# Another written order of casts, splits and gates over the first fourteen steps of a one-core decoder layer, with three scratch stores asked for later

## The chip, the cores and the metric

The kernel runs on one core of a Trainium2 chip. A core has a matrix engine (TensorE, PE in the profile), a vector engine (VectorE, DVE), a scalar engine (ScalarE, ACT), GpSimd (POOL) and a sync engine (SyncE, SP) that here only issues transfers. Each engine works through its own list of instructions in order, and semaphores are all that binds one engine to another. Transfers (DMA) are asked for by SP, or by POOL where a transfer adds to what lies at its destination, and run on 16 shared DMA engines. The metric is the device time of one execution in microseconds, as the median of three runs.

## The reference

One decoder layer on 512 tokens of 1024 features, in float32: a SwiGLU feed-forward block (FFN), a token-mixing part, a second FFN and a gated embedding. The edited code is the entry of the first FFN, with the embedding's projection `p @ ple_w_proj` that is computed ahead of it:

```python
h = h + 0.5 * swiglu(rmsnorm(h, ffn1_norm), w_gate, w_up, w_down)     # 1024 -> 2816 -> 1024
...
gate = sigmoid(rmsnorm(h, ple_norm) @ ple_w_gate + ple_b_gate)
h = h + gate * (p @ ple_w_proj)
# swiglu(x, w_gate, w_up, w_down) = (silu(x @ w_gate) * (x @ w_up)) @ w_down
```

Every product is made of three matmul passes over high and low parts (`whi`, `wlo` of the weights, `xfa`/`xfb` of the input), so that float32 accuracy is kept.

## The kernel before

**Steps.** The program is a list of steps. A step is one product on PE with the work that feeds it and the work that follows it. For each step a weight block of 128x1024 is loaded, cast on ACT (`whi`, line 537) and subtracted on DVE (`wlo`, line 541); the two together are called a split, the first half the cast, the second the low half. The first matmul of a product waits for the cast, the third for the low half. There are three buffers for `whi` and three for `wlo`.

**The entry.** Steps 0 and 1 are the embedding's projection (line 1231). Steps 2 to 5 are a plain group of 256 of the 2816 inner columns (line 847, 24 matmuls of 512 columns each). From step 6 on, groups of 256 inner columns are computed in a form of Strassen's with seven products a group (line 753, 24 matmuls of 256 columns each). Group 1 has steps 6 to 11 and 13; group 2 begins with step 12 and goes on with 14, 15 and so on. Some weight blocks are sums of blocks: two are made by adding transfers from POOL (lines 768 and 771, into `raw` and `s1`), two by a DVE addition in place (line 763). Step 7 uses the `raw` that a POOL transfer added to, step 9 the sum `rawb + s1`, step 11 `s1`, step 13 the same `rawb` after a second addition.

**What follows a product.** The plain group's gate is formed by `plain_gate` (DVE line 869, ACT line 871, into `g`) and its result by `plain_finish` (DVE lines 877 and 879). In group 1, `gate_sum` (line 904) reads a finished accumulator and writes the gate buffer `G`; `gate` multiplies by the norm's factor (line 909) and applies silu on ACT (line 911); `times_r` (line 915) and `finish` (line 920) follow. The second `gate_sum` reads the accumulator `a` that step 11 has just finished, and step 13 writes into that same accumulator again, so step 13's first matmul waits for it.

**Other work in the entry.** The input is scaled and split into `xfa` and `xfb`, with sums and differences of blocks (lines 633 to 687). The norm's squares are taken from four row blocks of x (line 390), then a chain of small DVE instructions gives the factor per token (lines 240 to 246), and a product spreads it (line 343); ACT keeps it as `rall` (line 349). The embedding's eight tiles are copied out of the accumulators (line 1241) and stored to a scratch tensor `emb_dram` (line 1186). Their buffers `rawd` lie where `G` lies later, so the first write to `G` waits for the `rawd` stores to have landed.

**What sets the order.** PE, ACT, DVE and SP run in the order in which a planner (`run`) writes the instructions. For the entry, that order is a string, `ENTRY`: a name such as `split7` runs the cast and low half of step 7, `split7:1` only its next piece, `after11` what follows product 11, `load9` the transfers tied to step 9. A suffix `.1` or `.2` names a further task of that step. All tasks not named run afterwards in the planner's default order. Each engine's list is what is left of this sequence when the other engines' pieces are taken out.

Of the kernel before, what the change touches and what calls it, by code (L numbers as in the profile page):

```python
# [50 lines left out]
ENTRY = """  # L51
load0 load1 load1.1 load2 load3 load3.1 load4 load5 split0 split1 split1.1 load6 load6.1
product0 split2 load7 product1 after1:1 after0 split3 split3.1:6 split4.1:3 split3.1:1
split4.1:1 split3.1 split4.1 split5.1:1 load8 after1:1 product2 split4.2:1 split4.2:1 split5.1:1
after1 split4 split4.2 split6.2:2 load9 product3 split5:1 split5.2:1 split5 split5.1 split6.1
after4:1 split5.2 split6.2:1 after4 split6.2:1 split5.3 product4 split6 split6.2:1 split6.2
product5 after4.1 split7 split7.1 product6 split8:1 sums9 after5:1 split8 after6 after5:2
split9:2 split10.1:1 after5 product7 split10.1:1 split9 product8 split10.1:1 after7
split10 split10.1 load12 product9 split11 load14 product10 after9 after9.1 after10
after10.1:1 split12 product11 after11 split13  # L60
"""

BUFS = {
# [43 lines left out]
def layer_kernel(ctx: ExitStack, tc: tile.TileContext, a: dict, out: bass.AP):  # L107
# [7 lines left out]
    def open_pool(name, side):  # L115
        pools[name] = tc.alloc_tile_pool(name=name, bufs=1, side=side, reuse_waits="tile")
        home.update(dict.fromkeys(HOMES[name].split(), name))

    def close_pool(*names):
        for name in names:  # L120
            pools.pop(name).release()
# [362 lines left out]
    def listed(fns):  # L484
        return list(fns) if isinstance(fns, (list, tuple)) else [fns] if fns else []

    def also(step, what, fn):

        if what == "after":
            step.after = (listed(step.after[0] if step.after else ()) + [fn],) + tuple(step.after[1:])  # L490
        else:
            setattr(step, what, listed(getattr(step, what)) + [fn])
# [223 lines left out]
    def splitter(name, x):  # L716

        x += [None] * ND

        def done(d, tok=slice(0, T)):  # L720
            x[d] = scaled_split(h, name, d, tok, x[d])

        return done
# [457 lines left out]
    emb_dram = dram.tile([P, ND, T], F32, name="emb_dram", tag="emb_dram")  # L1181
    pe, stores = [], {}

    def store_embedding():
        for d in (4, 6, 0, 2, 3):
            nc.sync.dma_start(*stores[d])

    def embedding(q):
# [67 lines left out]
    steps, mix_norm = swiglu(  # L1256
        "ffn1", x_ffn1, ffn1_norm,
        lambda: (close_pool("ffn1_entry"), open_pool("ffn1_g", "left")),
        lambda: (close_pool("ffn1_g"), open_pool("mix_x", "left")),
        splitter("mix_norm", x_mix), 1,  # L1260
    )
    steps = [embedding(q) for q in range(2)] + steps
# [11 lines left out]

    also(steps[1], "split", lambda: Early.x(early, 0))
    also(steps[3], "split", lambda: Early.x(early, 1))
    also(steps[9], "load", store_embedding)
    also(steps[4], "split", lambda: Early.t(early, 3))
    also(steps[4], "split", lambda: Early.t(early, 2))
    also(steps[5], "split", lambda: ffn1_norm.add(0, 1, 2))  # L1280
# [607 lines left out]
    for n, d in enumerate(D_ORDER):  # L1888
# [11 lines left out]
    steps, ple_norm = swiglu(  # L1900
        "ffn2", x_ffn2, norm, lambda: open_pool("ffn2_g", "right"),
        lambda: (close_pool("ffn2_g"), open_pool("ple_x", "right")), splitter("ple_norm", x_ple), 0,
    )
# [297 lines left out]
```

## Time and profile before

| | us |
|---|---|
| median of 3 runs (lowest, highest) | 1015.03 (1014.21, 1016.19) |
| the profiled execution's own time | 1015.65 |
| its span, first to last instruction | 1013.9 |
| PE busy in the span | 1003.9 |
| DVE busy, ACT busy | 845.3, 580.6 |

The profile is one execution, with a page of totals and views of the trace. In a timeline row stand the start, the duration, the engine, the line, the operation, output and inputs by tile name, and the count of instructions; in square brackets the engine's idle time just ahead and what ended it. The granted TensorE clock is 1.000 in the whole span.

### The profile page before, as it was taken

To read this page: it belongs to the slowest core of one execution; us is meant where nothing else is said; L and a number is where in the kernel's file an instruction comes from. 1 tells how busy PE (TensorE), PEld (TensorE's weight loads), DVE (VectorE), ACT (ScalarE), POOL (GpSimd) and SP (SyncE) were. 2 spreads that over 40 slices of the span, in tenths; PEclk is the share of its full clock that TensorE was granted. 3 is DMA by queue.
4 is the path that set the end of the run, shared out by engine and by line. 5 is a ranking of instruction groups with operands and counts; after the bars stand their busy time and mean duration, and the time that the engine had idled before them with its cause. 6 is when DMAs were issued, how large, how long until landed. Compare 5 with 4: busy or idle time off the path is not lost.

```text
span 1013.9 us, 18331 instructions
## 1 busy us (share of the span) xinstructions
PE 1003.9 (99%) x7464; PEld 948.4 (94%) x7464; DVE 845.3 (83%) x1116; ACT 580.6 (57%) x783; POOL 134.5 (13%) x141
## 2 busy tenths in 40 slices
PE   9999999999999999999999999999999999999997
PEld 7899999999999899888888888899999999999987
DVE  7988888889988897776999757778888888988886
ACT  6755555556667474575754434455545546665765
POOL 0101001002311000144233100101011000330101
PEclk9999999999999999999999999999999999999999
DMA  8977767748972333444432233746777756995512
GB/s 334 330 205 206 197 193 205 207 146 223 205 176 64 95 114 98 152 154 131 130 121 84 104 104 130 216 120 186 201 208 194 181 167 207 215 211 137 167 63 84
DMA packets 51333, 168.90 MB, mean 167 GB/s; under 512 B 5808, under 2 KB 6576, under 8 KB 51248
## 3 DMA queue, kind: packets, MB, share of 16 engines
q1 hardware_dynamic: 39584, 125.71, 36.2%
q0 software_dynamic: 11520, 41.95, 22.3%
q8 instruction: 58, 0.95, 0.4%
q14 instruction: 27, 0.22, 0.1%
q10 hardware_dynamic: 144, 0.07, 0.0%
HBM read 163.44 MB, written 4.26 MB: 165 GB/s over the span
## 4 chain that ended last, share of the span: by engine, by line
PE 88%; DVE 6%; DMA 3%; issue 1%; ACT 1%; SPq 0%; DVEq 0%; ACTq 0%
PE mm L753 20%; PE a L753 15%; PE a L1139 8%; PE mm L231 6%; PE sm L217 6%; PE mm L1139 5%; PE sm L1139 5%; PE mm L217 5%; PE sm L231 4%; PE a L217 4%; PE a L231 3%; DVE wlo L541 1%; DMA s<-in_ffn_gu 1%; DMA raw<-in_ffn_gu 1%; PE sm L847 1%
## 5 line engine op out<-in xcount | busy, mean ns | idle before, releaser
L541 DVE TENSOR_TENSOR wlo<-raw,whi 128x1024 fp32r<-128x1024 f32 (+2 forms) x162 | 199.4, 1231 | 58.3 <-ACT whi L537 58.1
L537 ACT CAST whi<-raw 128x1024 fp32r<-128x1024 f32 (+2 forms) x162 | 166.2, 1031 | 135.5 <-DVE raw L763 30.6
L753 PE MATMUL mm<-xfb,whi 128*128 128x256 f32 x960 | 163.9, 275 | 0.0
L753 PEld LDWEIGHTS mm<-xfb,whi 128*128 128x128 f32 x960 | 145.5, 192 | 0.0
L753 PE MATMUL mm<-xfb,wlo 128*128 128x256 f32 x480 | 132.1, 275 | 0.2 <-DVE wlo L541 0.2
L537 ACT CAST whi<-rawb 128x1024 fp32r<-128x1024 f32 x76 | 79.6, 1048 | 63.3 <-DVE rawb L763 29.5
L541 DVE TENSOR_TENSOR wlo<-rawb,whi 128x1024 fp32r<-128x1024 f32 x76 | 92.9, 1222 | 21.5 <-ACT whi L537 20.9
L753 PE MATMUL a<-xfb,whi 128*128 128x256 f32 x640 | 109.4, 275 | 0.0
L753 PEld LDWEIGHTS a<-xfb,whi 128*128 128x128 f32 x640 | 97.0, 192 | 0.0
L753 PEld LDWEIGHTS mm<-xfb,wlo 128*128 128x128 f32 x480 | 92.2, 192 | 0.4 <-DVE wlo L541 0.4
L753 PE MATMUL a<-xfb,wlo 128*128 128x256 f32 x320 | 88.1, 275 | 0.0
L1139 PE MATMUL a<-xfb,whi 128*128 128x256 f32 x480 | 80.7, 275 | 0.0
L1139 PEld LDWEIGHTS a<-xfb,whi 128*128 128x128 f32 x480 | 73.0, 192 | 0.0
L768 POOL DMA_DIRECT2D raw<-in_ffn_gu x20 | 17.3, 864 | 398.5 <-DMA raw<-in_ffn_gu 154.5
L217 PE MATMUL sm<-x,whi 128*128 128x512 f32 x224 | 68.3, 387 | 0.0
L1139 PE MATMUL a<-xfb,wlo 128*128 128x256 f32 x240 | 66.0, 275 | 0.0
L911 ACT ACTIVATE G<-G 128x512 f32<-128x512 f32 x40 | 25.3, 633 | 65.4 <-DVE G L909 64.1
L753 PEld LDWEIGHTS a<-xfb,wlo 128*128 128x128 f32 x320 | 61.4, 192 | 0.1
L753 PE MATMUL a<-xfa,whi 128*128 128x256 f32 x320 | 54.7, 275 | 0.1
L753 PE MATMUL mm<-xfa,whi 128*128 128x256 f32 x320 | 54.8, 275 | 0.0
L1139 PE MATMUL mm<-xfb,whi 128*128 128x256 f32 x320 | 53.8, 275 | 0.0
L1139 PE MATMUL sm<-xfb,whi 128*128 128x256 f32 x320 | 53.8, 275 | 0.0
(428 smaller groups left out, 2604.6 us busy)
## 6 DMA issues: line engine op xcount, KB each, us to landing
raw<-in_ffn_gu SPq DMA_DIRECT2D x56, 512.0 KB, 4.9
rawb<-in_ffn_gu SPq DMA_DIRECT2D x32, 512.0 KB, 8.8
raw<-in_w_in SPq DMA_DIRECT2D x28, 512.0 KB, 3.6
s<-in_ffn_gu SPq DMA_DIRECT2D x20, 512.0 KB, 5.7
raw<-in_ffn_gu POOLq DMA_DIRECT2D x20, 512.0 KB, 5.8
s<-in_ffn_gu POOLq DMA_DIRECT2D x20, 512.0 KB, 9.7
rawb<-in_ffn_dw POOLq DMA_DIRECT2D x18, 512.0 KB, 7.9
raw<-in_w_out SPq DMA_DIRECT2D x16, 512.0 KB, 3.2
```

The source lines that it names most:

```text
L217: nc.tensor.matmul(ps, w, turned(x), start=first and n == 0, stop=last and n == 2, skip_group_check=True)
L231: nc.tensor.matmul(ps[:, tok], wt[:, c], turned(xt[:, tok]), start=first and k == i == 0, stop=last and k == len(xs) - 1 and i == len(by_p ...
L537: nc.scalar.copy(self.hi[:, c], self.raw[:, c])
L541: nc.vector.tensor_tensor(self.lo[:, c], self.raw[:, c], self.hi[:, c].bitcast(F32), ALU.subtract)
L753: nc.tensor.matmul(o, wt[:, c], turned(xt), start=fresh and p == m == n == 0, stop=last and n == 2, skip_group_check=True,)
L768: nc.gpsimd.dma_start(w21.raw, self.src[0], accum_op=ALU.add)
L847: nc.tensor.matmul(ps, (whi, whi, wlo)[n][:, c], t[:, 0:2, n % 2].rearrange("p s (b i) -> p s i b", b=2), start=not lower and p == n == 0, ...
L911: nc.scalar.activation(t, t, AF.Silu)
L1139: nc.tensor.matmul(o, wt[:, c], xt, start=i in (1, 7) and t == jj == n == d % 2 == 0, stop=t == nt - 1 and jj == 1 and d % 2 == 1 and n == ...
```

## The change

The string `ENTRY` is rewritten from step 1's place to step 13's. The products stand in the same order. On ACT and DVE the splits of steps 4 to 9 and of step 12 and 13 are written earlier relative to the work around them: relative to the norm's squares, to the last of the input's sums (`split5.3`), to the plain group's gate (`after5`) and finish (`split10.1`), and to group 1's gates (`after10`, `after11`). Of the five stores to `emb_dram`, the two of 256 KB stay with step 9's loads, and the other three of 512 KB are tied to step 14's loads (`load14.1`) instead. No instruction is added or taken away.

```diff
-split4.1:1 split3.1 split4.1 split5.1:1 load8 after1:1 product2 split4.2:1 split4.2:1 split5.1:1
-after1 split4 split4.2 split6.2:2 load9 product3 split5:1 split5.2:1 split5 split5.1 split6.1
-after4:1 split5.2 split6.2:1 after4 split6.2:1 split5.3 product4 split6 split6.2:1 split6.2
-product5 after4.1 split7 split7.1 product6 split8:1 sums9 after5:1 split8 after6 after5:2
-split9:2 split10.1:1 after5 product7 split10.1:1 split9 product8 split10.1:1 after7
-split10 split10.1 load12 product9 split11 load14 product10 after9 after9.1 after10
-after10.1:1 split12 product11 after11 split13
+split4.1:1 split3.1 split4.1 split5.1:1 load8 after1:1 product2 split4.2:1 split4.2:1 split4
+split5.1:1 after1 split4.2 split6.2:2 load9 product3 split5:1 split5.2:1 split5 split5.1 split6.1
+after4:1 split6.2:1 split6:1 after4 split6.2:1 split6 product4 split6.2 split5.2 split5.3:1
+product5 after4.1 split7:1 split8:1 split5.3:1 split7 split8 split7.1 product6 sums9 after5:1 after6
+split9 split5.3 after5:2 product7 split10 after7 after5 split10.1:2 product8 split11:1 load12 split11
+product9 after9 split12:1 split12 split10.1 load14 load14.1 product10 after9.1 split13:1 after10 split13
+after10.1:1 product11 after11
...
-    def store_embedding():
-        for d in (4, 6, 0, 2, 3):
+    def store_embedding(*ds):
+        for d in ds:
             nc.sync.dma_start(*stores[d])
...
-    also(steps[9], "load", store_embedding)
+    also(steps[9], "load", lambda: store_embedding(2, 3))
+    also(steps[14], "load", lambda: store_embedding(4, 6, 0))
```

What the rewritten string makes of the engines' lists is shown at three places. The first is ACT ahead of step 4, as a piece of the difference; `whi_318` was and `whi_314` is the cast of step 4's weights, and line 390 takes the squares of a row block of x.

```order
 L390 ACTIVATE whix_174,rtok_281<-whix_174 128x1024
 L1241 COPY rawd_250<-mm_223 128x512
+L537 CAST whi_314<-raw_140 128x1024
 L390 ACTIVATE wlox_176,rtok_281<-wlox_176 128x1024
-L537 CAST whi_318<-raw_140 128x1024
 L668 CAST xfb_100<-ghi_271 128x512
```

Step 4's cast now stands ahead of the second row block's squares instead of behind them.

The second place is DVE from step 11's low half (`wlo_588` before, `wlo_557` now) to step 14's (`wlo_697` in both), with the semaphores that each row waits for. First the list before, in which `wlo_634` is step 12's low half and `wlo_663` step 13's:

```order
L541 TENSOR_TENSOR wlo_588<-s_57_217,whi_587 128x1024 [waits PE_49,Activation_49]
L763 TENSOR_TENSOR rawb_172<-rawb_172,rawb_283 128x1024
L904 TENSOR_TENSOR G_630<-mm_503,u_116_623 128x2x256 [waits DMAHW4_49,DMAHW5_49,PE_49,Activation_49]
L909 SCALAR_TENSOR_TENSOR G_630<-G_630,rall_489 128x2x256 [waits DVE_49]
L541 TENSOR_TENSOR wlo_634<-raw_110_561,whi_633 128x1024 [waits DMAHW1_49,Activation_49]
L904 TENSOR_TENSOR G_630<-a_98_459,p_107_554 128x2x256 [waits PE_49]
L541 TENSOR_TENSOR wlo_663<-rawb_172,whi_662 128x1024 [waits Activation_49]
L915 SCALAR_TENSOR_TENSOR G_630<-G_630,rall_489 128x2x256 [waits Activation_49]
L541 TENSOR_TENSOR wlo_697<-raw_591,whi_696 128x1024 [waits DMASW2_49,Activation_49]
```

Then the list now, in which `wlo_589` is step 12's low half and `wlo_631` step 13's; DMAHW3 and DMAHW2 are the semaphores of the two `rawd` stores:

```order
L541 TENSOR_TENSOR wlo_557<-s_57_217,whi_556 128x1024 [waits PE_49,Activation_49]
L541 TENSOR_TENSOR wlo_589<-raw_112_559,whi_588 128x1024 [waits DMAHW6_49,PE_49,Activation_49]
L877 SCALAR_TENSOR_TENSOR g_487<-g_487,rall_485 128x512
L879 TENSOR_TENSOR g_487<-g_487,a_82_332 128x512 [waits DVE_49]
L763 TENSOR_TENSOR rawb_172<-rawb_172,rawb_283 128x1024
L904 TENSOR_TENSOR G_637<-mm_498,u_113_586 128x2x256 [waits DMAHW3_49,DMAHW2_49,PE_49]
L541 TENSOR_TENSOR wlo_631<-rawb_172,whi_630 128x1024 [waits Activation_49]
L909 SCALAR_TENSOR_TENSOR G_637<-G_637,rall_485 128x2x256 [waits DVE_49]
L904 TENSOR_TENSOR G_637<-a_100_458,p_109_527 128x2x256 [waits PE_49]
L915 SCALAR_TENSOR_TENSOR G_637<-G_637,rall_485 128x2x256 [waits Activation_49]
L541 TENSOR_TENSOR wlo_697<-raw_594,whi_696 128x1024 [waits DMASW2_49,Activation_49]
```

Step 12's low half moved ahead of the plain group's finish (lines 877, 879), of the second addition (line 763) and of the first gate sum; step 13's low half moved ahead of line 909 and of the second gate sum, the line-904 row that reads the accumulator `a`.

The third place is SP's list of transfers, before:

```order
L511 DMA rawb_283<-in_ffn_gu 128x1024
L1186 DMA emb_dram<-rawd_250 128x1024
L1186 DMA emb_dram<-rawd_315 128x1024
L1186 DMA emb_dram<-embt_252 128x1024
L1186 DMA emb_dram<-p_65_255 128x512
L1186 DMA emb_dram<-u_66_257 128x512
L511 DMA raw_110_561<-in_ffn_gu 128x1024
L511 DMA raw_591<-in_ffn_gu 128x1024
L770 DMA s_114_594<-in_ffn_gu 128x1024
L511 DMA raw_597<-in_ffn_gu 128x1024
L511 DMA rawb_667<-in_ffn_gu 128x1024
```

and now:

```order
L1186 DMA emb_dram<-p_65_255 128x512
L1186 DMA emb_dram<-u_66_257 128x512
L511 DMA raw_112_559<-in_ffn_gu 128x1024
L511 DMA raw_594<-in_ffn_gu 128x1024
L770 DMA s_117_597<-in_ffn_gu 128x1024
L511 DMA raw_600<-in_ffn_gu 128x1024
L1186 DMA emb_dram<-rawd_250 128x1024
L1186 DMA emb_dram<-rawd_319 128x1024
L1186 DMA emb_dram<-embt_252 128x1024
```

The three large stores moved behind group 2's first four loads; the last of these, `raw_600`, overwrites the buffer that step 7's split reads.

## The prediction

> **What bounds the kernel now.** I read the page's totals first, then the chain of waits, then the stretches of the entry.
>
> ```profile
> span 1013.9 us, 18331 instructions
> PE 1003.9 (99%) x7464; PEld 948.4 (94%) x7464; DVE 845.3 (83%) x1116; ACT 580.6 (57%) x783; POOL 134.5 (13%) x141
> PE 88%; DVE 6%; DMA 3%; issue 1%; ACT 1%; SPq 0%; DVEq 0%; ACTq 0%
> ...
> 20.00:40.00 20.00, 19.07 (x90) 16.12 (x89) 19.17 (x38) 14.89 (x24) 1.92 (x2) 1.00 1.04 367
> 40.00:60.00 20.00, 19.82 (x177) 19.63 (x176) 18.79 (x23) 12.40 (x16) 2.53 (x3) 1.00 0.90 270
> 80.00:100.00 20.00, 20.00 (x182) 20.00 (x181) 17.33 (x21) 10.90 (x14) 2.57 (x3) 1.00 0.79 209
> ```
>
> In a row of stretches the busy times are PE, weight load, DVE, ACT, POOL; then clock, DMA share and GB/s. PE is the bound of the whole program and never idle from 80 to 100, so a shift of PE that stands at 80 us stays to the end. In the entry DVE is as full as PE: 19.17 of 20 us from 20 to 40, 18.79 from 40 to 60, DMA at 0.90 to 1.04 beside it. A new order adds no work and takes none away, so it can win only PE's gaps here, and lose by what DVE idles. PE's gaps, from its timeline:
>
> ```profile
> 26.59 0.59 PE L847 MATMUL a<-xfa,whi 128*128 128x512 f32 x2
> 27.02 0.38 PE L847 MATMUL a<-xfa,wlo 128*128 128x512 f32 x1
> 27.77 0.70 PE L847 MATMUL sm<-xfb,whi 128*128 128x512 f32 x2 [0.37 <-ACT whi L537]
> 29.02 0.48 PE L847 MATMUL sm<-xfb,wlo 128*128 128x512 f32 x1 [0.56 <-DVE wlo L541]
> 33.88 0.59 PE L847 MATMUL mm<-xfb,whi 128*128 128x512 f32 x2
> 44.88 0.39 PE L753 MATMUL mm<-xfb,whi 128*128 128x256 f32 x2
> 45.45 0.38 PE L753 MATMUL mm<-xfb,wlo 128*128 128x256 f32 x1 [0.18 <-DVE wlo L541]
> 45.66 0.39 PE L753 MATMUL mm<-xfb,whi 128*128 128x256 f32 x2
> 58.45 0.39 PE L753 MATMUL mm<-xfa,whi 128*128 128x256 f32 x2
> 58.79 0.39 PE L753 MATMUL a<-xfb,whi 128*128 128x256 f32 x2
> 64.47 0.38 PE L753 MATMUL a<-xfb,wlo 128*128 128x256 f32 x1
> ```
>
> Two matmuls of 512 columns take 27.02 - 26.59 = 0.43 us, so step 4's 24 take 5.18. Step 4 was due at 27.24 and step 5 at 32.42; step 5 came at 33.88. Step 4 loses **1.46 us**, more than the 0.93 shown as idle, since the pipeline has to fill twice. Three matmuls of 256 columns take 0.34 (58.45 to 58.79), so after 44.88 the fourth of step 8 was due at 45.22 and came at 45.66: **0.44 us**. That is all there is to win, 1.9 us. Rows 58.79 (step 13's first matmul) and 64.47 (step 15's first on a low half) are the marks against which the new order is held.
>
> **The change part by part.** Step 4's gap comes from ACT:
>
> ```profile
> 25.63 1.06 ACT L390 ACTIVATE wlox<-wlox 128x1024 f32<-128x1024 f32 x1 [1.00 <-DMA wlox<-in_x_rows]
> 26.68 1.03 ACT L537 CAST whi<-raw 128x1024 fp32r<-128x1024 f32 x1
> 27.62 0.61 ACT L668 CAST xfb<-ghi 128x512 fp32r<-128x512 f32 x1
> 27.75 1.23 DVE L541 TENSOR_TENSOR wlo<-raw,whi 128x1024 fp32r<-128x1024 f32 x1 [0.45 <-ACT whi L537]
> ```
>
> The cast waited behind squares that waited 1.00 us for a transfer. Written ahead of them it fits into that idle time, the low half starts near 26.0, and the 1.46 us go, with 0.45 us of DVE idle time. The squares lose nothing: their data come at 25.63 anyway. The last addition of the input's sums (two rows of line 671) now runs behind step 9's low half, which frees 1.2 us of DVE ahead of step 7. So DVE, which reached step 7's low half at 40.72, now reaches it at 40.72 - 0.45 - 1.20 = 39.07. What it meets there:
>
> ```profile
> 38.93 1.05 ACT L537 CAST whi<-raw 128x1024 fp32r<-128x1024 f32 x1 [1.56 <-DMA raw<-in_ffn_gu]
> 40.72 1.22 DVE L541 TENSOR_TENSOR wlo<-raw,whi 128x1024 fp32r<-128x1024 f32 x1
> 42.44 1.23 DVE L763 TENSOR_TENSOR rawb<-rawb,s 128x1024 f32<-128x1024 f32 x1 [0.50 <-DMA s<-in_ffn_gu]
> 43.58 0.68 DVE L869 TENSOR_TENSOR g<-sm,rall 128x512 f32<-128x512 f32 x1
> 44.18 1.22 DVE L541 TENSOR_TENSOR wlo<-rawb,whi 128x1024 fp32r<-128x1024 f32 x1
> ...
> 42.81 0.59 ACT L883 COPY a<-mm 128x512 f32<-128x512 f32 x1
> ```
>
> Step 7's cast waits for POOL's adding transfer, not for ACT. Cast to low half is 1.07 us (26.68 to 27.75), a DVE row of 1024 columns occupies 1.14 (42.44 to 43.58), one of 512 0.60. I take the transfer 0.2 us later than before (below), so cast at 39.13, low half of step 7 at 40.20: DVE has idled 1.1 us. Step 8's low half follows at 41.34, line 763 at 42.48. ACT from step 7's cast to the end of line 883 took 43.40 - 38.93 = 4.47 us and now has one line 668 of 0.6 more: 44.20, less the 0.1 it idled, 44.1. There step 9's cast starts, and its low half at 45.17: DVE, free at 44.22, has idled again, 0.95 us.
>
> From there DVE does not stop. Its rows and their spacing:
>
> ```profile
> 47.05 0.68 DVE L877 SCALAR_TENSOR_TENSOR g<-g,rall 128x512 f32<-128x512 f32 x1
> 47.76 0.69 DVE L879 TENSOR_TENSOR g<-g,mm 128x512 f32<-128x512 f32 x1
> 51.84 1.22 DVE L763 TENSOR_TENSOR rawb<-rawb,rawb 128x1024 f32<-128x1024 f32 x1
> 53.62 0.69 DVE L904 TENSOR_TENSOR G<-mm,u 128x512 f32<-128x512 f32 x1 [0.57 <-issue]
> 55.08 0.65 ACT L911 ACTIVATE G<-G 128x512 f32<-128x512 f32 x1 [0.52 <-DVE G L909]
> 56.25 0.69 DVE L904 TENSOR_TENSOR G<-a,p 128x512 f32<-128x512 f32 x1
> 58.59 1.22 DVE L541 TENSOR_TENSOR wlo<-raw,whi 128x1024 fp32r<-128x1024 f32 x1
> 63.19 1.23 DVE L541 TENSOR_TENSOR wlo<-raw,whi 128x1024 fp32r<-128x1024 f32 x1 [0.25 <-ACT whi L537]
> ```
>
> Lines 877 and 879 together take 0.71 + 0.60 = 1.31. Low half of step 9, two of line 671, line 869, low half of 10, 877 and 879, low halves of 11 and 12, 877 and 879: 1.14 + 1.20 + 0.60 + 1.14 + 1.31 + 2.28 + 1.31 = 8.98. So line 763, which ran at 51.84, now starts at 54.15 and ends at 55.38. Step 13's cast needs it; low half at 55.42 + 1.07 = 56.49, after the first line 904. Behind it line 909 at 57.63 and the second line 904 at 58.23, done at 58.92. It ran at 56.25 and was no one's wait; now step 13, which writes the accumulator that it reads, starts behind it at about 58.95, against 58.79. PE would have come there 1.9 us earlier less some 0.5 lost at step 7, whose third matmul follows its low half by 1.27 (27.75 to 29.02): **what was won is spent at step 13.**
>
> It goes on. Line 909 ends at 58.32; silu follows on ACT (0.55 to the next row), then step 14's cast at 58.9, its low half at 59.97, against 58.59: 1.4 us late. From here both lists are the same up to step 15's low half: 63.19 becomes 64.6, and step 15's third matmul goes from 64.47 to 65.85. Nothing behind it is tighter, DVE having 2.7 us of 20 to spare from 80 on. The sum against the profiled execution: 1015.65 + 1.35 = 1017.0, of which 1013.9 is span; its run lies 0.6 above the median, so against 1015.03 it is **1016.4**.
>
> The unknown is the transfers:
>
> ```profile
> 41.97 0.33 SPq L511 DMA_DIRECT2D raw<-in_ffn_gu x1
> emb_dram<-rawd SPq DMA_DIRECT2D x2, 512.0 KB, 9.7
> q0 software_dynamic: 286, 1.05, 70.0%
> q1 hardware_dynamic: 378, 0.99, 36.0%
> 27.00:34.00 7.00, 6.07 (x27) 4.68 (x26) 6.40 (x13) 6.34 (x11) 1.92 (x2) 1.00 1.02 411
> ```
>
> The queue rows are of 34.4 to 41.9 us, when the two adding transfers (q0) ran beside stores (q1). They moved 0.99 MB of q1 in 36% of 7.5 us, 2.7 us; the loads that take the stores' place go at 411 GB/s, 2.4 us for as much, but in 4 KB pieces, so one more of q1 may come between every two of q0. Later by half a load, 0.6 us, is the far bound; earlier by the 1.3 us of q1's time that falls to one adding transfer is the other, where group 2's loads, now asked for sooner and no longer behind the three stores, are through before. Later moves the sum up to +1.8; earlier lets DVE meet step 7's cast without waiting, from 38.0 on, and stops there: 39.13 - 38.0 = 1.1 less, **+0.3**. I take 0.2 later because the bytes ahead of them in the queue hardly differ.
>
> The stores themselves are hidden: SP asks for them behind the load that ran at 41.97, now near 41.5 when step 7's low half has ended, and at 9.7 us they land near 51. `G` is first written at 55.3, and 55.9 would do, as step 13's low half comes only at 56.49.
>
> [...]
>
> **The rivals.** *The gain is kept*: step 13 finds its accumulator read in time, as 56.25 was before. Then 1.9 less the 0.5 at step 7 or less: 1013.1 to 1013.6. For it speaks that the splits themselves come earlier; against it the 8.98 us of DVE rows ahead of line 763. 0.08. *DVE only loses its gap*: the adding transfers are early and ACT is no wait for step 9; DVE runs through, 0.45 us sooner: 1014.6, 0.12. *Early transfers alone*, step 9 still behind ACT: 1015.03 + 0.3 = 1015.3, 0.20. *The stores hold G*: they stand behind group 2's two adding transfers, which now are asked for just then. Two such took 7.5 us; 41.5 + 7.5 + 9.7 = 58.7, and from 55.9 on each microsecond counts: +2.8 on the forecast, 1019.2. Against it, 9.7 was measured with adding transfers beside it. 0.08. *The forecast*: 0.52, by itself 1015.8 to 1017.0.
>
> **How the numbers follow.** The likeliest is 1016.4. From 1014.3 to 1017.6 lie the second and third rival and the forecast with its late bound, some 0.84. The median of three runs can tell 0.2%, 2.0 us, from no change. Faster by more than that needs the first rival in full, below 1013.0: 0.04. Slower needs the stores (0.08) or a forecast with late transfers, above 1017.06 (0.09): 0.17. No change that can be told: 0.79.
>
> **What would show it.** Right: no PE idle time at step 4, DVE idle ahead of step 7's and step 9's low halves, PE waiting at step 13 for line 904 and at step 15 for ACT or DVE, step 15's third matmul near 65.8. If line 904 runs ahead of 57, step 13's part is wrong; if step 7's cast starts by 38, the transfers were the error; if line 904's first row waits for a store, the last rival holds.

## The result, and the profile after

The changed kernel takes 1016.07 us (median of 22 executions, 1015.58 to 1016.97); the kernel before, timed beside it, takes 1014.80 (22 executions, 1014.13 to 1016.19). The ratio is 1.0012, with an interval of 1.0007 to 1.0018: slower by a little over 1 us, less than the 2 us that the prediction set as what can be told, but clear of its interval with so many executions. The prediction was 1016.4. The profiled execution took 1016.36.

First the page's span and the row of stretches of the changed kernel (columns as in the prediction's):

```profile
span 1014.6 us, 18334 instructions
...
20.00:40.00 20.00, 20.00 (x104) 17.79 (x103) 18.93 (x37) 14.39 (x23) 1.92 (x2) 1.00 1.03 357
40.00:60.00 20.00, 18.67 (x163) 18.18 (x163) 18.28 (x22) 12.11 (x17) 1.69 (x2) 1.00 0.88 262
60.00:80.00 20.00, 19.31 (x171) 18.93 (x170) 16.77 (x19) 9.56 (x12) 2.52 (x3) 1.00 0.70 193
```

PE, idle for 0.93 us between 20 and 40 before, is never idle there now. Its idle time has moved to 40 to 60 (1.33 us) and 60 to 80 (0.69). (The page counts three instructions more than before, 18334 for 18331; the counts of PE, DVE, ACT and POOL are the same.) Its timeline shows the places:

```profile
26.92 0.59 PE L847 MATMUL sm<-xfb,whi 128*128 128x512 f32 x2
...
32.10 0.60 PE L847 MATMUL mm<-xfb,whi 128*128 128x512 f32 x2
...
56.90 0.28 PE L753 MATMUL mm<-xfa,wlo 128*128 128x256 f32 x1
58.44 0.46 PE L753 MATMUL a<-xfb,whi 128*128 128x256 f32 x2 [1.27 <-ACT G L911]
...
63.76 0.28 PE L753 MATMUL mm<-xfb,wlo 128*128 128x256 f32 x1
64.44 0.49 PE L753 MATMUL a<-xfb,whi 128*128 128x256 f32 x2 [0.40 <-ACT a L883]
65.22 0.38 PE L753 MATMUL a<-xfb,wlo 128*128 128x256 f32 x1 [0.29 <-DVE wlo L541]
...
1007.74 1.04 PE L2009 MATMUL mm<-ident,h 128*128 128x128 f32 x8
```

Step 4 now lasts 32.10 - 26.92 = 5.18 us, its full-speed time: the 1.46 us are gone. Step 13 was due one spacing of 0.11 after 56.90, at 57.01, and starts at 58.44: 1.43 lost. Step 15 was due at 63.87 and starts at 64.44; its third matmul was due two spacings, 0.22, later, at 64.66, and starts at 65.22: 0.57 and 0.56. The rows behind these waits, on ACT and DVE:

```profile
38.48 1.05 ACT L537 CAST whi<-raw 128x1024 fp32r<-128x1024 f32 x1 [5.59 <-DMA raw<-in_ffn_gu]
39.56 1.23 DVE L541 TENSOR_TENSOR wlo<-raw,whi 128x1024 fp32r<-128x1024 f32 x1 [0.66 <-ACT whi L537]
41.97 1.23 DVE L763 TENSOR_TENSOR rawb<-rawb,s 128x1024 f32<-128x1024 f32 x1
44.45 1.23 DVE L541 TENSOR_TENSOR wlo<-rawb,whi 128x1024 fp32r<-128x1024 f32 x1 [0.66 <-ACT whi L537]
53.46 1.22 DVE L763 TENSOR_TENSOR rawb<-rawb,rawb 128x1024 f32<-128x1024 f32 x1
...
57.61 0.69 DVE L904 TENSOR_TENSOR G<-a,p 128x512 f32<-128x512 f32 x1
57.73 0.63 ACT L911 ACTIVATE G<-G 128x512 f32<-128x512 f32 x1 [1.89 <-DVE G L909]
59.34 1.23 DVE L541 TENSOR_TENSOR wlo<-raw,whi 128x1024 fp32r<-128x1024 f32 x1 [0.25 <-ACT whi L537]
63.81 0.58 ACT L883 COPY a<-mm 128x512 f32<-128x512 f32 x1
63.93 1.23 DVE L541 TENSOR_TENSOR wlo<-raw,whi 128x1024 fp32r<-128x1024 f32 x1 [0.24 <-ACT whi L537]
```

The second line 904, at 56.25 before, runs at 57.61; step 14's low half, at 58.59 before, at 59.34; step 15's, at 63.19 before, at 63.93. Two of the rows put an end to a wait of PE that they may only stand next to: the silu of line 911 ends at 58.36, line 904 at 58.30, and step 13 starts at 58.44. The experiment on which row ends the wait at step 13 separates the two.

### The profile page after: what moved, and what is told of

It is laid out like the page before. It is cut to its first block, busy times and chain, and to the rows that moved or that the text cites. A ratio compares the mean times of both kernels' runs of the same rounds, so it can differ in the third digit from the quotient of the medians.

```text
span 1014.6 us, 18334 instructions
## 1 busy us (share of the span) xinstructions
PE 1004.2 (99%) x7464; PEld 949.1 (94%) x7464; DVE 846.0 (83%) x1116; ACT 580.5 (57%) x783; POOL 134.2 (13%) x141
## 4 chain that ended last, share of the span: by engine, by line
PE 87%; DVE 6%; DMA 3%; ACT 1%; issue 1%; SPq 0%; DVEq 0%; ACTq 0%; POOLq 0%
PE mm L753 20%; PE a L753 15%; PE a L1139 8%; PE mm L231 6%; PE sm L217 6%; PE mm L1139 5%; PE sm L1139 5%; PE mm L217 5%; PE sm L231 4%; PE a L217 4%; PE a L231 3%; DMA raw<-in_ffn_gu 2%; DVE wlo L541 2%; DMA h<-in_x 1%; PE sm L847 1%
```

## The experiments

The theory on trial: PE's gap at step 4 is closed, but the order behind it makes PE wait at steps 13 and 15 for what DVE and ACT are asked to do before. The main rivals: the gap's worth is kept and something else costs more; the stores that were moved cost the time; the wait at step 13 is for the silu. (A run whose text is a line longer or shorter has its line numbers shifted by one or two: line 537 can be 536 or 538.)

### One part alone: step 4's cast

```diff
 (the kernel before)
-split4.1:1 split3.1 split4.1 split5.1:1 load8 after1:1 product2 split4.2:1 split4.2:1 split5.1:1
-after1 split4 split4.2 split6.2:2 load9 product3 ...
+split4.1:1 split3.1 split4.1 split5.1:1 load8 after1:1 product2 split4.2:1 split4.2:1 split4
+split5.1:1 after1 split4.2 split6.2:2 load9 product3 ...
```

> The kernel before with one thing of the change: step 4's cast ahead of the second row block's squares. My theory (the entry is set by DVE's list): step 4's 1.46 us go, PE reaches step 5 that much sooner, but line 763 waited until 42.44 for the second adding transfer and step 8's low half stands behind it on DVE at 44.18, so step 8's third matmul stays near 45.45 and nothing is left: 1014.8, within 0.3. Rival, that a gap closed on PE is kept: step 8's third matmul near 44.0 and 1013.3 to 1014.3.

Measured: 1015.12 us (11 executions), ratio to the kernel before 1.0002, interval 0.9993 to 1.0010; 0.3 above what was expected, and not the rival's gain. PE's and DVE's timeline:

```profile
38.78 0.38 PE L753 MATMUL mm<-xfa,wlo 128*128 128x256 f32 x1 [0.72 <-DVE wlo L541]
42.09 1.22 DVE L763 TENSOR_TENSOR rawb<-rawb,s 128x1024 f32<-128x1024 f32 x1 [1.03 <-DMA s<-in_ffn_gu]
45.11 0.38 PE L753 MATMUL mm<-xfb,wlo 128*128 128x256 f32 x1 [0.70 <-DVE wlo L541]
...
1006.64 1.04 PE L2008 MATMUL mm<-ident,h 128*128 128x128 f32 x8
```

Step 4's gap is gone and nothing is won. PE, early, waits for the low half of step 6 (0.72), which stands behind other rows of DVE, and again for that of step 8 (0.70), which stands behind line 763, and that waits for the second adding transfer. In this execution step 4's gap is not on the path; the interval alone, about 1 us either way, could not say so, and the distances of the next experiment do.

### The same end from the same row: the kernel before once more

> The kernel before, unchanged, for a second profile of it. Theory: its end counts from line 763 at step 8, which waits for the second adding transfer; the last group of eight matmuls starts 964.55 us behind that row, as in the profile before and in the one with step 4's cast moved, whenever the transfer lands. Rival: the distance differs by more than 0.2 us.

Measured: 1014.71 us (10 executions).

```profile
41.51 1.23 DVE L763 TENSOR_TENSOR rawb<-rawb,s 128x1024 f32<-128x1024 f32 x1 [0.47 <-DMA s<-in_ffn_gu]
...
1006.04 1.04 PE L2008 MATMUL mm<-ident,h 128*128 128x128 f32 x8
```

From line 763 to the last eight matmuls are 1006.04 - 41.51 = 964.53 us here, 1006.64 - 42.09 = 964.55 in the experiment above, and, with the row 42.44 of the prediction and the last group at 1006.99,

```profile
1006.99 1.04 PE L2008 MATMUL mm<-ident,h 128*128 128x128 f32 x8
```

964.55 in the profile before. The row moves by 0.93 us from one execution to another, as the transfer lands, and the end moves with it. Step 4 itself loses 1.46 us in the profile before, 0.86 in the second one (step 4 starts at 26.94, step 5 at 32.98) and nothing with its cast moved; the distance stays.

### One part alone: the stores

```diff
 (the kernel before)
-split10 split10.1 load12 product9 split11 load14 product10 ...
+split10 split10.1 load12 product9 split11 load14 load14.1 product10 ...
-    also(steps[9], "load", store_embedding)
+    also(steps[9], "load", lambda: store_embedding(2, 3))
+    also(steps[14], "load", lambda: store_embedding(4, 6, 0))
```

> The kernel before with the other part of the change alone: the three large stores behind group 2's first four loads, the written order otherwise as it was. My theory: the stores are not what made the change slower; the adding transfers land 0.4 us sooner, line 763 starts at 42.0 instead of 42.44, step 8's gap of 0.44 shrinks, 1014.4 to 1014.8. Rival, that the stores cost the time (G waits for them, or group 2's transfers collide): 1015.5 or more, with the first line 904 waiting for a transfer.

Measured: 1015.23 us (12 executions), from 1014.58 to 1019.05; ratio 1.0010, interval 1.0000 to 1.0020. My number was missed and half of the rival's was right. Four of the twelve executions took 1017.1 or more, where the highest of 35 of the kernel before was 1016.22, and in the profiled execution (1019.05) `G` does wait for a store. The tile's view and DVE's timeline:

```profile
L1186 SPq DMA_DIRECT2D emb_dram<-rawd x2: 422/423/424, 41.8 to 42.2; - x2
...
DMA to landing us min/median/max: 8.0/10.6/13.2
...
55.54 0.69 DVE L904 TENSOR_TENSOR G<-mm,u 128x512 f32<-128x512 f32 x1 [3.16 <-PE a L753]
```

The second `rawd` store, asked for at 42.2, lands 13.2 us later at 55.4; line 904 starts at 55.54. The row names PE, but the product that it reads was done when PE began the next one at 52.70, and in the profile before line 904 starts 0.25 us behind that point (53.37 and 53.62). So PE's part of the wait ends near 52.95, and the other 2.6 us are the store's. In the changed kernel the same two stores, asked for at 41.2 and 41.7, landed within 7.0 us,

```profile
L1186 SPq DMA_DIRECT2D emb_dram<-rawd x2: 423/423/423, 41.2 to 41.7; - x2
...
DMA to landing us min/median/max: 5.1/6.0/7.0
```

by 48.7, and line 904 came only at 54.59. In the old order line 904 comes 1 to 2 us earlier (53.62 and 52.70 in the two profiles of the kernel before) and meets the store when it is late.

### The change without its stores

```diff
 (the changed kernel)
-product9 after9 split12:1 split12 split10.1 load14 load14.1 product10 ...
+product9 after9 split12:1 split12 split10.1 load14 product10 ...
-    also(steps[9], "load", lambda: store_embedding(2, 3))
-    also(steps[14], "load", lambda: store_embedding(4, 6, 0))
+    also(steps[9], "load", lambda: store_embedding(4, 6, 0, 2, 3))
```

> The changed kernel with the three large stores back with step 9's loads. My theory: step 7's cast starts with the first adding transfer, 0.45 us later than in the changed kernel (38.9 instead of 38.48), DVE's list from there moves by it, step 13 starts near 58.9 and step 15's third matmul near 65.7: 1016.5. Rival, that the stores cost the time: 1015 or less. Rival, that transfers set nothing here: 1016.1.

Measured: 1016.16 us (11 executions), ratio to before 1.0013 (1.0005 to 1.0022), the same as the change with its stores moved.

```profile
37.98 1.05 ACT L537 CAST whi<-raw 128x1024 fp32r<-128x1024 f32 x1 [5.14 <-PE sm L343]
...
57.94 0.46 PE L753 MATMUL a<-xfb,whi 128*128 128x256 f32 x2 [1.27 <-ACT G L911]
...
1007.25 1.04 PE L2008 MATMUL mm<-ident,h 128*128 128x128 f32 x8
```

The stores are not the loss, and no help that these numbers can tell. My reason for 1016.5 fell: with the stores back the first adding transfer landed not later but 0.5 us sooner. The time is that of the second rival, that transfers set nothing; against it stands the distance: from step 7's cast to step 13 are 57.94 - 37.98 = 19.96 us, and 58.44 - 38.48 = 19.96 in the changed kernel; to the last group 969.27 and 969.26. (The row of the cast names PE here; in the trace the transfer's last piece lands at 37.88, 0.10 ahead of the cast, as in the changed kernel, 38.38 and 38.48.) In the changed order the end counts from the landing of the first adding transfer.

### Part of the plain group's finish later

```diff
 (the changed kernel)
-product9 after9 split12:1 split12 split10.1 load14 load14.1 product10 after9.1 split13:1 after10 split13
-after10.1:1 product11 after11
+product9 after9 split12:1 split12 load14 load14.1 product10 after9.1 split13:1 after10 split10.1
+split13 after10.1:1 product11 after11
```

> The changed kernel with the second half of the plain group's finish (lines 877 and 879, 1.31 us) moved from ahead of line 763 to behind the first line 904, where DVE waits 0.59 us for step 13's cast. My theory: line 763 starts 1.31 us sooner, the second line 904 ends near 57.6 instead of 58.30, step 13's first matmul follows at 57.65 instead of 58.44, and the whole list of DVE behind it is 0.67 sooner: 1015.4. Rival, that step 13 and 15 wait for something that this list does not set: step 13 at 58.4 as now, 1016.1.

Measured: 1015.64 us (11 executions), 0.43 under the changed kernel; ratio to before 1.0004 (0.9995 to 1.0013).

```profile
38.91 1.04 ACT L537 CAST whi<-raw 128x1024 fp32r<-128x1024 f32 x1 [5.73 <-DMA raw<-in_ffn_gu]
...
58.19 0.46 PE L753 MATMUL a<-xfb,whi 128*128 128x256 f32 x2 [0.58 <-ACT G L911]
```

Step 13 follows step 7's cast by 19.28 us instead of 19.96: 0.68 sooner, where 0.67 was expected. The transfer landed 0.43 later in this execution, which hides it in the absolute times, and the median of 1015.64 is between the 1015.4 expected and the rival's 1016.1. The order of DVE's rows does set step 13.

### Which row ends the wait at step 13

```diff
 (the changed kernel)
-after10.1:1 product11 after11
+product11 after11 after10.1:1
```

> The changed kernel with the second line 904 (it reads the accumulator) ahead of line 909 on DVE, nothing else. The profile names the silu on ACT (line 911) as what ended PE's wait at step 13; it ends 0.06 us behind the second line 904, so either could be it. My theory, line 904: counted from step 7's cast, to stay clear of when the transfer lands, line 904 comes 0.6 sooner and step 13 starts 19.3 us behind that cast instead of 19.96; the silu and step 14's cast come 0.6 later, so that step 14 loses some, and step 15's third matmul comes 0.5 or so later than now: 1016.4 to 1016.8. Rival, silu: step 13 starts 0.6 us later, 20.6 behind step 7's cast.

Measured: 1016.88 us (10 executions), ratio 1.0014 (1.0005 to 1.0023).

```profile
38.46 1.06 ACT L537 CAST whi<-raw 128x1024 fp32r<-128x1024 f32 x1 [5.27 <-DMA raw<-in_ffn_gu]
...
57.95 0.46 PE L753 MATMUL a<-xfb,whi 128*128 128x256 f32 x2 [0.78 <-DVE G L904]
61.31 0.38 PE L753 MATMUL mm<-xfb,wlo 128*128 128x256 f32 x1 [0.23 <-DVE wlo L541]
65.13 0.49 PE L753 MATMUL a<-xfb,whi 128*128 128x256 f32 x2 [1.10 <-ACT a L883]
```

Step 13 starts 19.49 us behind step 7's cast, 0.47 sooner, though the silu comes later; the row now names line 904. (0.6 was expected; step 9's low half came 0.13 later behind the cast, 6.10 us for 5.97.) So it was line 904 all along, which reads the accumulator. And the gain is given back further on: PE waits 0.23 at step 14 and 1.10 instead of 0.40 at step 15, since silu, casts and the copy of line 883 stand behind one another on ACT.

### Leaving out each adding transfer

The first of the two, on the kernel with only step 4's cast moved:

```diff
+                if self.j > 1:
-                nc.gpsimd.dma_start(self.s1, self.src[3], accum_op=ALU.add)
+                    nc.gpsimd.dma_start(self.s1, self.src[3], accum_op=ALU.add)
```

> The kernel before with step 4's cast ahead of the squares, and group 1's second adding transfer (into s1, line 771) left out, so that steps 9 and 11 compute with half of their weight sum. My theory: closing step 4's gap brought nothing by itself because line 763 then waited 1.03 us for this transfer and step 8's low half stood behind it. Without it line 763 follows step 7's low half at once, 1.0 sooner, step 8's third matmul no longer waits (0.87), and that part of the 1.46 is kept: 1013.9 to 1014.3. Rival, that something else takes the gain of step 4 back: as with the transfer, 1014.8 to 1015.1.

Measured: 1014.90 us (11 executions), ratio 1.0000 (0.9991 to 1.0009). The theory's number fell; the time is the rival's.

```profile
38.97 1.05 ACT L537 CAST whi<-raw 128x1024 fp32r<-128x1024 f32 x1 [2.48 <-DMA raw<-in_ffn_gu]
40.03 1.28 ACT L1284 ACT_TABLE_LOAD   x1
...
41.44 1.03 ACT L537 CAST whi<-rawb 128x1024 fp32r<-128x1024 f32 x1
42.37 0.58 ACT L349 COPY rall<-sm 128x512 f32<-128x512 f32 x1
...
41.19 1.22 DVE L763 TENSOR_TENSOR rawb<-rawb,s 128x1024 f32<-128x1024 f32 x1
42.99 0.69 DVE L870 TENSOR_TENSOR g<-sm,rall 128x512 f32<-128x512 f32 x1 [0.58 <-ACT rall L349]
```

Line 763 runs 0.9 us sooner, as expected. But the row between it and step 8's low half (the gate, line 869, here 870) then waits for `rall`, and ACT copies that only behind step 7's cast, the table load and step 8's cast, so again behind the first adding transfer. In the order before, step 8's low half stands behind both transfers. By the first one's way the gate runs 4.02 us behind step 7's cast (42.99 - 38.97), which in the profile before is 42.95, where by the second's it ran at 43.58; with only step 4's cast moved it is 42.32 for 43.24. So the second transfer came last by 0.6 to 0.9 us, and the first one's way stands just behind it. Without the second transfer line 763 is no longer the row from which the end counts (965.20 us here), and step 8's low half still is: 962.79 us to the last group (43.60 to 1006.39), 962.81 in the profile before (44.18 to 1006.99).

The other, on the changed kernel, with the same edit on the line of `w21.raw`:

> The changed kernel with group 1's first adding transfer (into raw, line 768) left out, so that step 7 computes with half of its weight sum. My theory: in the changed order DVE's list from step 7 on starts when this transfer lands. Without it DVE does not wait 0.66 us ahead of step 7's low half (38.9 instead of 39.56); line 763 and step 9's cast come 0.7 to 0.9 sooner, the second line 904 and step 13's first matmul with them, near 57.6 instead of 58.44: 1015.1 to 1015.5. Rival, that the landing of this transfer sets nothing behind step 7: step 13 at 58.4 and 1016.1.

Measured: 1015.71 us (11 executions), 0.36 under the changed kernel; neither the 1015.1 to 1015.5 expected nor the rival's 1016.1.

```profile
57.85 0.46 PE L753 MATMUL a<-xfb,whi 128*128 128x256 f32 x2 [1.05 <-ACT G L912]
```

Step 13 starts 0.59 sooner than in the changed kernel, not 0.84, and PE still waits 1.05 us for it. DVE, which reached step 7's low half at 38.9, runs it at 38.96 and not 39.56, 0.60 sooner, and step 13 follows by 18.89 us, 18.88 in the changed kernel. The transfer decides where DVE's list begins; that step 13 is late is the list's own length.

### Another order behind step 8

```diff
 (the changed kernel)
-split9 split5.3 after5:2 product7 split10 after7 after5 split10.1:2 product8 split11:1 load12 split11
-product9 after9 split12:1 split12 split10.1 load14 load14.1 product10 after9.1 split13:1 after10 split13
-after10.1:1 product11 after11
+split9:1 split5.3:1 split9 split5.3 after5:2 product7 split10 after7 after5 split10.1:2 product8 split11:1 load12 split11
+product9 after9 split12:1 split12 load14 load14.1 product10 after9.1 split13:1 after10 split10.1 split14:1
+split13 product11 after11 split14 load18 product12 after12 sums15 cast15 after10.1:1 product13 split15
+load20 product14 split16
```

> The changed kernel up to step 8, with another order from there on: one row of line 671 in the 0.66 us that DVE waits for step 9's cast; the second half of the plain group's finish behind the first line 904; step 14's cast ahead of the silu; the second line 904 and the low halves of 14, 15 and 16 ahead of the first group's gates (lines 909, 915, 920); the copy that seeds group 2's accumulator (line 883) and step 15's sum right behind step 12. My theory, that steps 13 and 15 wait only because DVE's and ACT's rows stand in this order: both waits go, some 2.4 to 2.9 us: 1013.2 to 1013.7, and PE has no idle time between step 8 and 80 us. Rival, that DVE has no time left here: the gates that are put off make PE wait between 64 and 80 us, 1015 to 1016.

Measured: 1013.43 us (12 executions), ratio to before 0.9982 (0.9974 to 0.9991): faster than both kernels. Its row of stretches:

```profile
40.00:60.00 20.00, 20.00 (x182) 20.00 (x181) 18.70 (x22) 12.73 (x18) 2.46 (x3) 1.00 0.93 279
60.00:80.00 20.00, 20.00 (x182) 20.00 (x181) 18.11 (x21) 10.34 (x15) 2.63 (x4) 1.00 0.75 193
```

PE is never idle from 40 to 80 in this execution. DVE, busy for 35.05 us of these 40 in the changed kernel (18.28 and 16.77), is busy for 36.81: the work that PE waited for was possible, it stood in the wrong place. Several rows were moved at once, so what each of them is worth is not shown. Two of the twelve executions took 1354 and 2009 us, so it was run again:

> The kernel with the new order behind step 8 once more, since two of its executions took 1354 and 2009 us. Theory: those two have nothing to do with the order, the median is 1013.2 to 1013.8 again and none is over 1016. Rival: the order brings an occasional long wait, and some are over 1100 again.

Measured: 1013.61 us (11 executions, 1013.00 to 1014.07), ratio 0.9982 (0.9973 to 0.9991). The two long ones did not come again; what they were isn't known.

With the stores at step 9 as before the change:

> The same as the kernel with the new order behind step 8, with the three large stores back with step 9's loads. The first line 904 comes about 2 us sooner in this order, near 52.5, and so nearer to when the later stores land. My theory: no difference of medians over 0.3 us, since neither place of the stores sets step 7's cast or line 904 in most executions; 1013.2 to 1013.7, with fewer late ones than with the stores late. Rival, that the later stores are worth something: over 0.5 us slower than with them late.

Measured: 1013.78 us (11 executions, 1013.08 to 1014.75), ratio 0.9985 (0.9977 to 0.9994). That is 0.35 us over the first run of the new order and 0.17 over the second: no difference that these numbers can tell, and the fewer late executions that were expected don't show either. In this profile and in that of the second run the transfer landed late (step 7's cast at 39.30 and 39.01), and PE idles at step 7's third matmul, 0.77 and 0.25 us, for the low half behind it. From that cast to the last group are 966.58 and 966.55 us, against 969.26 in the changed kernel: the order behind step 8 is worth 2.7 us, where 2.4 to 2.9 was expected.

And the later part of that order on the kernel before, to see whether the change's early part is worth something under it:

```diff
 (the kernel before)
-after10.1:1 split12 product11 after11 split13
+split14:1 split12 product11 after11 split13 split14 load18 product12 after12 sums15
+cast15 after10.1:1 product13 split15 load20 product14 split16
```

> The kernel before with the new order only from step 12 on (casts and low halves of 14 to 16, the second line 904 and the seed ahead of the gates), all ahead of that as it was. My theory: before, PE is held at step 8 by the second adding transfer (line 763) and loses only about 0.2 at step 15, so only that can go: 1014.3 to 1014.8. Rival, that the new order is what is worth something and the change's early part nothing: as fast as the changed kernel with it, 1013.2 to 1013.7.

Measured: 1014.45 us (11 executions), ratio 0.9993 (0.9985 to 1.0002), as expected. Against the same executions of the kernel before (1014.97) that is 0.5 us less, not clear of its interval, where the whole new order on top of the change gave 1.5. About 1.0 of it comes only with the change's early part. Which piece of that part it is, no run separates, and this profile shows that step 4's cast can be one:

```profile
28.25 0.48 PE L848 MATMUL sm<-xfb,wlo 128*128 128x512 f32 x1 [0.69 <-DVE wlo L542]
...
33.10 0.59 PE L848 MATMUL mm<-xfb,whi 128*128 128x512 f32 x2
```

Step 4 starts at 26.97 here and was due to end at 32.15; step 5 starts at 33.10, 0.95 us late. Behind it PE loses nothing: from step 5's first matmul to the last group are 972.42 us (1005.52 at the end), the same as in the profile of the new order, where PE never idles from 20 to 80 us (972.44), and 973.11 in the profile before. The transfer landed early in this execution (step 7's cast at 37.92, line 763 without a wait), so here step 4's gap is on the path. In the profile before PE loses another 0.7 us behind step 5, and there it is the transfer that holds it.

## Why the prediction was right, and where it was not

**Step 4** went as forecast: 5.18 us, no idle time. That its 1.46 us were 0.53 more than the idle time shown is in the rows of the profile before: ahead of each of the two waits the last matmul ends 0.59 - 0.43 = 0.16 us later than the next was due, and the row behind each wait lasts 0.11 and 0.10 longer (0.70 for 0.59, 0.48 for 0.38).

**"That is all there is to win, 1.9 us"** took the two gaps as two gains, and they are not. Closing step 4's gap alone wins nothing where the kernel is held at step 8 by line 763 and its transfer; 964.55 us from there to the last group, three times. The change also writes the low halves of steps 7 and 8 ahead of line 763, and the two together did win: step 13 would have been due at 57.01, 1.78 sooner than 58.79 before. No run has the low halves moved alone. Part of the 1.78 is the first transfer, which landed 0.45 sooner (step 7's cast at 38.48, 38.93 before): step 8's first matmul, at 43.51, follows the copy of line 883, which ends at 43.45 and stands on ACT behind that cast. At equal landings that is 1.3, where 1.9 less 0.5 was forecast: the size holds, the sum of two separate gaps behind it does not.

**The waits ahead of the low halves of steps 7 and 9** are there, 0.66 and 0.66 us, for 1.1 and 0.95 forecast. The transfer, which I took 0.2 us later than before, came 0.45 sooner (step 7's cast at 38.48, not 39.13). That the loads' larger pieces could hold it up, by as much as 0.6 us, was my estimate; q1 moved 0.61 MB in 170 packets from 34.4 to 41.9 us here, for 0.99 MB in 378 before, and no delay came with it in this execution. That the stores' place shifts it is not borne out: the cast starts at 37.95 to 39.01 over six profiles with the stores late, and at 37.92 to 39.30 over seven with the stores at step 9. The earliest and the latest are in the last two kernels of the experiments, both with the stores in the old place:

```profile
37.92 1.05 ACT L538 CAST whi<-raw 128x1024 fp32r<-128x1024 f32 x1 [1.32 <-DMA raw<-in_ffn_gu]
```

on the kernel before with the later part of the new order, and

```profile
39.30 1.05 ACT L536 CAST whi<-raw 128x1024 fp32r<-128x1024 f32 x1 [6.23 <-DMA raw<-in_ffn_gu]
```

on the changed one with the new order.

**The 8.98 us of DVE rows, and what follows them**, were right to some hundredths, counted from that cast. Line 763: 54.15 - 39.13 = 15.02 forecast, 53.46 - 38.48 = 14.98 measured. Step 13's first matmul: 19.82 forecast, 19.96 measured. Step 15's third matmul: 26.72 forecast, 26.74 measured. That step 13 waits for the second line 904 is shown by the exchange of two rows (0.47 sooner) and by the finish put off (0.68 sooner), against the row's own label.

**At step 15** I named ACT or DVE; it is both in turn, 0.57 us for the copy of line 883, which I had not named, and 0.56 for the low half.

**The size.** The prediction added 1.35 us; its own two rows, 65.85 and 64.47, give 1.38. Of the 1.35 us, 0.2 were the late transfer, which did not come. With equal landings the forecast is 1.15; the traces give, with step 7's cast at 38.93 as in the profile before, 38.93 + 969.26 = 1008.19 for the last group, against 1006.99 in the profile before: 1.20. The medians differ by 1.27.

**The stores** that `G` waits for land by 48.7 and hold nothing in the changed order, as forecast (51 was the guess). The rival that they hold `G` was not empty, though: in the old order, where line 904 comes 1 to 2 us sooner, it cost 2.6 us of DVE's time in the one execution that was profiled.

**The second rival**, that DVE only loses its gap of 0.45 us, ends at 1014.6. The first experiment closes that gap, and its ratio to before is 1.0002; the interval would leave room for 0.45 us, but in the trace DVE waits 0.53 us longer at line 763 instead (1.03 for 0.50). The gap that counted was the wait of line 763 for a transfer.

## What to carry to other kernels

A gap on the bounding engine is worth something only if the next place where that engine waits moves with it: follow it to the next wait, and see what sets that one. An anchor helps: where the distance from one row to the program's end is the same to a few hundredths over several executions, that row, or one that it moves with, sets the end, and changes are best counted from it, since its own start may move by a microsecond. When work is put off on an engine that is nearly full, look for what is queued behind it and read last by the bound engine, here a read of an accumulator; put off first what nobody reads soon.

## What the runs showed of the hardware

In the execution of the kernel with only the stores moved, the granted clock fell after PE's wait ahead of 58.15. PE's timeline and the row of stretches:

```profile
58.15 0.38 PE L753 MATMUL mm<-xfa,wlo 128*128 128x256 f32 x1 [2.38 <-DVE wlo L541]
...
58.92 0.28 PE L753 MATMUL mm<-xfa,wlo 128*128 128x256 f32 x1
...
59.38 0.42 PE L753 MATMUL mm<-xfa,wlo 128*128 128x256 f32 x1
...
61.94 0.42 PE L753 MATMUL mm<-xfa,wlo 128*128 128x256 f32 x1
...
62.56 0.28 PE L753 MATMUL a<-xfb,wlo 128*128 128x256 f32 x1
...
55.00:58.00 3.00, 0.76 (x7) 0.57 (x6) 2.43 (x3) 1.01 (x2) 0.00 (x0) 1.00 1.03 415
58.00:60.00 2.00, 1.85 (x12) 1.85 (x13) 2.00 (x4) 0.56 (x1) 0.00 (x0) 0.78 0.57 229
60.00:62.00 2.00, 2.00 (x12) 2.00 (x11) 2.00 (x3) 0.00 (x0) 1.32 (x2) 0.50 0.40 37
62.00:64.00 2.00, 2.00 (x17) 2.00 (x17) 1.90 (x4) 0.67 (x2) 0.37 (x1) 0.87 0.69 129
64.00:66.00 2.00, 2.00 (x20) 2.00 (x19) 1.75 (x2) 2.00 (x3) 0.00 (x0) 1.00 0.91 238
```

The clock is 0.78, 0.50 and 0.87 over 2 us each, 1.00 before and after; a matmul of 256 columns takes 0.28 us at 58.92, 0.42 at 59.38 and 61.94, and 0.28 again at 62.56. So 0.44 + 1.00 + 0.26 = 1.7 us of PE's time are lost on top of the wait of 2.38, and the drop comes when PE is at work again. From step 8's low half to the last group are 966.82 us here (43.51 to 1010.33), 4.0 more than in the profile before, which is about the two together. In the profile of the changed kernel the wait of 1.27 us ahead of 58.44 left the clock at 1.00 in the rows of 40 to 60 and 60 to 80. That the wait is what set the drop off is inferred from this one execution.

Step 7's cast starts 0.10 us behind the landing of the first adding transfer's last piece, in the kernel before (38.83 and 38.93), in the changed one (38.38 and 38.48) and in that with its stores back (37.88 and 37.98). The cast is between 37.92 and 39.30 us in the profiles that have this transfer. Two executions of the same kernel differ by 1.06 us (37.95 and 39.01, the new order) and by 0.86 (38.93 and 38.07, the kernel before). In the one profile without the second adding transfer the first landed no sooner (the cast at 38.97). What moves it is open.
